# Four single PSUM banks instead of two bank pairs for the down products of a Strassen-style SwiGLU

## The chip, the cores and the metric

The kernel runs on one core of one Trainium2 chip. The metric is the device time of one execution, in microseconds (us). Three runs of the kernel before gave 1541.43, 1543.85 and 1544.39 us, so the median is 1543.85 us.

## The reference, cut to what matters

The program is one decoder layer on 1024 tokens of width 1024: modulation from a condition vector, a mixer of sparse attention and causal pooling, a layer norm, a gated feed-forward (SwiGLU) and a second layer norm. The change lies in the feed-forward:

```python
def swiglu(h, w_gate, w_up, w_down):
    return (jax.nn.silu(h @ w_gate) * (h @ w_up)) @ w_down

x = layer_norm(ALPHA * x + gate2 * ffn, ln2_g[l], ln2_b[l])
```

The hidden width is 2816, which is 11 times 256.

## The kernel before

**Operands.** All matrix work has float32 quality: an operand is split into a high part (rounded by ScalarE) and a low part (the rest, subtracted on VectorE or GpSimd), and a product is three matmuls, high by high, high by low and low by high (the table `SPLITS`).

**Passes.** The feed-forward goes over the 11 groups of 256 hidden columns. Line 1544 is the loop of the nine middle passes, `for p in range(1, NFP - 1)`. A pass computes the gate products ("g") of group p, the down products ("d") of group p-1, and the up products ("u") of group p. Each of the three is done as a two-by-two block product in seven steps instead of eight, in the manner of Strassen and Winograd. The sums of blocks that this needs are formed on GpSimd and VectorE. I write g0 to g6, d0 to d6 and u0 to u6 for the steps. The order in which a pass is written down is the string on line 60, `DOWN_AT = "gdgdgdggdgdgdd"`, followed by the seven up steps:

```
g0 d0 g1 d1 g2 d2 g3 g4 d3 g5 d4 g6 d5 d6   u0 u1 u2 u3 u4 u5 u6
```

**A gate or up step** (`gu_step`, line 1376) is 12 matmuls into a single PSUM bank of the pool `ps1` (four banks, tiles named `gu`). Step 3 is split into two halves of six, around step 4.

**A down step** (`down_step`, line 1526) is four groups of three matmuls. Group i (0 to 3) takes 128 tokens of the activations and writes bank i. Behind each group VectorE adds bank i to a tile of the residual, `res_X` (an evacuation of 128x512). Steps d0, d2, d4 and d6 start fresh sums (the flag `new` in the table `DOWN` on line 1288). Steps d1, d3 and d5 go on summing in the banks of the step before them, after that step's sums have been read out:

```python
DOWN = (("A11", "B11", True, (22,)), ("A12", "B21", False, (11,)), ("S1", "T1", True, (22,)), ("A22", "T4", False, (-21,)),
        ("S3", "T3", True, (22,)), ("S4", "B22", False, (-12,)), ("S2", "T2", True, (22,)))
```

**The banks before.** The four banks come as two tiles of 1024 columns from the pool `ps2` (two buffers, `psB` on line 213). Groups 0 and 1 share the first tile, groups 2 and 3 the second. A matmul that writes a tile is made to wait for the VectorE read of that tile that stands ahead of it in the program, whichever half of the tile it read.

**Weights.** A step's weights are a block of 128x1024 (high and low part) in one of four slots, used in turn (`wblk_V` and `wblk_T`, two each). A block is made up to four steps ahead (`LEAD = 4`), and a slot is free when the matmuls that read it are done. The raw weights of a gate, down or up group lie in one of two buffers, `wraw_R` and `wraw_W`. When the last block of a group has been made, the SyncE queue issues the load of the group after next into the same buffer (`load_set`).

**Activations.** The u steps end in the seven operands of the next down steps, `act_W` and `act_R`, again high and low part (`act_split`, line 1370).

**Order.** In the attention stages the order on three engines is fixed by the program. From line 975 on (`pinned.clear()`) it is not: the build orders each engine's instructions by the dependencies and its own estimates. All of what follows lies behind that line. Every operation is issued through one helper, so the profile shows L159 for nearly all of them, and they are told apart by the names of their tiles: `dn` is a down sum, `gu` a gate or up sum.

Of the kernel before, what the change touches and what calls it, by code (L numbers as in the profile page):

```python
# [171 lines left out]
def decoder_layer_kernel(  # L172
# [16 lines left out]
        area[nm_] = at  # L189
        at += 4 * words  # L190
    nc.alloc_sbuf_tensor("arena", [P, (at - nc.sbuf_base) // 4], F32)
    ps2 = ctx.enter_context(tc.tile_pool(name="ps2", bufs=2, space=bass.MemoryType.PSUM))
    ps1 = ctx.enter_context(tc.tile_pool(name="ps1", bufs=4, space=bass.MemoryType.PSUM))

    def buf(where, off, n, name, dt=F32):
        return nc.alloc_sbuf_tensor_at(f"{name}_{where}{off}", [P, n], dt, offset=area[where] + 4 * off).ap()

    n_ps = [0]

    ps_ring = {"ps1": [], "ps2": []}  # L200

    def ps_tile(pool, tag, n, depth, nm):
        n_ps[0] += 1
        t = pool.tile([P, n], F32, tag=tag, name=f"{nm}_{n_ps[0]}")
        ring = ps_ring[tag]
        times.prev[t[:, 0:n].name] = ring[-depth] if len(ring) >= depth else None
        ring.append(t[:, 0:n].name)
        return t
# [4 lines left out]
    def psB(nm="pb"):  # L213
        return ps_tile(ps2, "ps2", 1024, 2, nm)
# [725 lines left out]
    for n_, (kind, a, b) in enumerate(groups):  # L940
        if n_ in PAIRS:
            pb = psB("pair")
# [184 lines left out]
    for n_, u in enumerate(units):  # L1127
        g, pr, i = u
# [178 lines left out]
    def block(n):  # L1307
        if n < 7:
            return FIRST[n]
        if n < len(blocks) - 8 or n >= len(blocks) - 4:  # L1310
            return RING[(n - 7) % NRING]
        return TOK[:, 1, n + 8 - len(blocks)]
# [50 lines left out]
    def use_blocks(n):  # L1363
        pos["used"] += n

        lead = LEAD + 4 if pos["used"] >= len(blocks) - 11 else LEAD
        while pos["made"] < min(pos["used"] + lead, len(blocks)):
            make_block()
# [63 lines left out]
    def gate_up(kind, act, after=None):  # L1432
        for n in range(7):
            gu_step(kind, n, 0, 4, act)
            if after is not None:
                after(n)
# [63 lines left out]
    def E(rc, i):  # L1500

        t = 7 - 2 * i if rc >= 20 else 6 - 2 * i
        return XR[t][:, 0:512] if rc % 10 == 1 else XR[t][:, 512:1024]
# [3 lines left out]
    def affine(n=0):  # L1507
        if todo:
            t = todo.pop(0)
            V.tensor_tensor(XR[t], XR[t], GR, ALU.mult)  # L1510
            (G if t in AFF_G else V).tensor_tensor(XR[t], XR[t], lnb, ALU.add)
            if t % 2 == 0:
                for to in (12, 21):
                    G.tensor_tensor(E(to, (7 - t) // 2), E(to, (7 - t) // 2), E(22, (7 - t) // 2), ALU.subtract)
            if not todo:
                SP.dma_start(GR, g2_d.to_broadcast([P, 1024]))
# [4 lines left out]
            affine()  # L1521
    gate_up("u", ACTS, lambda n: affine())

    bank = {}

    def down_step(p, n):
        a_, w_, new, (to,) = DOWN[n]
        wd_ = block(pos["used"])
        if new:
            pb = [psB("dn"), psB("dn")]  # L1530
            bank.update({i: pb[i // 2][:, (i % 2) * 512 : (i % 2 + 1) * 512] for i in range(4)})
        for i in range(4):
            for m, (a, b) in enumerate(SPLITS):
                T.matmul(bank[i], ACTS[a_][:, a * 512 + i * P : a * 512 + (i + 1) * P], wd_[:, b * 512 : (b + 1) * 512],
                         start=(new and m == 0), stop=(m == 2), skip_group_check=True)
            z = E(abs(to), i)
            op = ALU.add if to > 0 else ALU.subtract
            if p == 0 and (n == 0 or not new):
                V.scalar_tensor_tensor(z, z, float(np.float32(ALPHA)), bank[i], ALU.mult, op)
            else:  # L1540
                V.tensor_tensor(z, z, bank[i], op)
        use_blocks(1)

    for p in range(1, NFP - 1):
        n_g = n_d = 0
        for kind in DOWN_AT:
            if kind == "g":
                gu_step("g", n_g, 0, 4, None)
                n_g += 1
            else:  # L1550
                down_step(p - 1, n_d)
                n_d += 1
        gate_up("u", ACTS if p < NFP - 2 else PLAIN)
# [109 lines left out]
```

## Time and profile before

| what | value |
|---|---|
| median of three runs | 1543.85 us |
| time of the profiled execution | 1548.71 us |
| its span, first to last instruction | 1546.8 us |
| TensorE matmuls, busy | 1262.8 us (82%) |
| VectorE busy | 1059.8 us (69%) |
| GpSimd busy | 821.5 us (53%) |
| ScalarE busy | 609.6 us (39%) |
| mean granted TensorE clock | 0.893 |

Busy time is a sum over the whole span, and says nothing of which engine is waited for at a given place. For that one reads the waits (who waited for whom), the timeline (instructions of one engine in order of time, with the idle time ahead of each in square brackets and what ended it) and the chain of work that ended last. PE is TensorE, DVE is VectorE, ACT is ScalarE, POOL is GpSimd. The granted clock is a share of full speed.

### The profile page before, as it was taken

To read this page: it belongs to the slowest core of one execution; us is meant where nothing else is said; L and a number is where in the kernel's file an instruction comes from. 1 tells how busy PE (TensorE), PEld (TensorE's weight loads), DVE (VectorE), ACT (ScalarE), POOL (GpSimd) and SP (SyncE) were. 2 spreads that over 40 slices of the span, in tenths; PEclk is the share of its full clock that TensorE was granted. 3 is DMA by queue.
4 is the path that set the end of the run, shared out by engine and by line. 5 is a ranking of instruction groups with operands and counts; after the bars stand their busy time and mean duration, and the time that the engine had idled before them with its cause. 6 is when DMAs were issued, how large, how long until landed. Compare 5 with 4: busy or idle time off the path is not lost.

```text
span 1546.8 us, 16019 instructions
## 1 busy us (share of the span) xinstructions
PE 1262.8 (82%) x5462; PEld 965.7 (62%) x5462; DVE 1059.8 (69%) x1725; ACT 609.6 (39%) x1141; POOL 821.5 (53%) x779
## 2 busy tenths in 40 slices
PE   7888978677699799947787878787969696969886
PEld 6655666565366478746665656575757574747675
DVE  6898898999779847874555646464555555645478
ACT  2446516456577644633222232222323222323321
POOL 1573847574344532595455555545464646465547
PEclk9999989898699889968797979797979797979989
DMA  9520113010006641011110101010101020202012
GB/s 351 188 96 14 66 37 102 22 68 21 0 15 199 234 133 41 1 52 57 30 53 28 55 28 55 28 55 25 58 11 72 4 78 1 82 1 82 28 55 109
DMA packets 24999, 101.80 MB, mean 66 GB/s; under 512 B 3411, under 2 KB 3411, under 8 KB 20566
## 3 DMA queue, kind: packets, MB, share of 16 engines
q1 hardware_dynamic: 24918, 100.78, 18.4%
q8 instruction: 43, 0.70, 0.2%
q14 instruction: 38, 0.31, 0.1%
HBM read 92.38 MB, written 8.40 MB: 65 GB/s over the span
## 4 chain that ended last, share of the span: by engine, by line
PE 30%; DVE 27%; POOL 22%; issue 9%; DMA 6%; ACT 6%; SPq 0%; DVEq 0%; POOLq 0%; ACTq 0%
PE gu L159 13%; PE dn L159 11%; DVE junk_X L159 7%; POOL act_W L159 4%; POOL wraw_R L159 4%; POOL wraw_W L159 3%; DVE score_X L159 3%; DVE stat_C L159 2%; POOL res_X L159 2%; DMA wraw_R<-in_wd_dram 2%; DVE res_X L159 2%; PE o L159 2%; PE pT L159 2%; DMA wraw_W<-in_wd_dram 2%; POOL gtmp_V L159 1%
## 5 line engine op out<-in xcount | busy, mean ns | idle before, releaser
L159 PE MATMUL gu<-hr_H,wblk_V 128*128 128x512 f32 (+1 forms) x936 | 244.3, 407 | 22.2 <-POOL hr_H L159 13.2
L159 PE MATMUL gu<-hr_H,wblk_T 128*128 128x512 f32 (+1 forms) x924 | 235.1, 402 | 5.8 <-ACT gtmp_V L159 3.0
L159 PEld LDWEIGHTS gu<-hr_H,wblk_V 128*128 128x128 f32 x936 | 185.4, 202 | 63.0 <-POOL hr_H L159 13.7
L159 DVE TENSOR_TENSOR res_X<-res_X,dn 128x512 f32<-128x512 f32 (+1 forms) x253 | 169.7, 683 | 70.6 <-PE dn L159 70.3
L159 PEld LDWEIGHTS gu<-hr_H,wblk_T 128*128 128x128 f32 x924 | 180.9, 201 | 44.2 <-ACT gtmp_V L159 3.4
L159 PE MATMUL dn<-wblk_V,act_W 128*128 128x512 f32 x324 | 99.1, 440 | 74.2 <-DVE res_X L159 52.8
L159 PE MATMUL dn<-wblk_T,act_W 128*128 128x512 f32 x324 | 97.3, 436 | 60.7 <-DVE res_X L159 43.3
L159 PE MATMUL pj<-ws_W,hT_H 128*128 128x512 f32 x456 | 124.7, 422 | 18.7 <-DVE kr_K L159 6.5
L159 PEld LDWEIGHTS dn<-wblk_V,act_W 128*128 128x128 f32 x324 | 64.4, 209 | 101.4 <-DVE res_X L159 65.4
L159 POOL TENSOR_TENSOR wraw_R<-wraw_R 128x512 f32<-128x512 f32 x64 | 90.9, 1421 | 57.2 <-DVE wblk_T L159 23.1
L159 PEld LDWEIGHTS dn<-wblk_T,act_W 128*128 128x128 f32 x324 | 64.7, 208 | 86.3 <-DVE res_X L159 54.3
L159 PEld LDWEIGHTS pj<-ws_W,hT_H 128*128 128x128 f32 x456 | 88.9, 201 | 46.4 <-issue 16.7
L159 POOL TENSOR_TENSOR wraw_W<-wraw_W 128x512 f32<-128x512 f32 x60 | 82.5, 1375 | 46.9 <-DVE wblk_T L159 23.0
L159 POOL TENSOR_SCALAR sm_H<-sm_H,stat_X 128x1024 f32<-128x1024 f32 (+7 forms) x64 | 58.3, 923 | 73.7 <-DVE stat_X L159 58.4
L159 DVE TENSOR_TENSOR act_W<-gtmp_V,act_W 128x512 fp32r<-128x512 f32 x19 | 23.3, 1225 | 89.2 <-ACT act_W L159 89.2
L159 DVE TENSOR_SCALAR_CACHE_REDUCE junk_X<-keysD_T,colsD_X 128x1024 int16<-128x1024 int16 (+1 forms) x64 | 78.9, 1269 | 0.8
L159 ACT ACTIVATE wblk_V<-wraw_R 128x512 fp32r<-128x512 f32 x56 | 35.3, 632 | 101.8 <-PE dn L159 42.3
L159 ACT ACTIVATE wblk_V<-wraw_W 128x512 fp32r<-128x512 f32 x54 | 34.1, 631 | 100.3 <-PE dn L159 38.3
L159 ACT ACTIVATE wblk_T<-wraw_W 128x512 fp32r<-128x512 f32 x55 | 34.6, 630 | 95.8 <-PE dn L159 40.0
L159 ACT ACTIVATE act_W<-gtmp_V 128x512 fp32r<-128x512 f32 x48 | 29.3, 627 | 101.5 <-POOL gtmp_V L159 81.4
L159 ACT ACTIVATE wblk_T<-wraw_R 128x512 fp32r<-128x512 f32 x53 | 33.2, 630 | 88.3 <-PE dn L159 34.9
L159 POOL TENSOR_TENSOR wraw_R<-wraw_R,gr_G 128x512 f32<-128x512 f32 x24 | 32.9, 1380 | 62.1 <-DMA wraw_R<-in_wd_dram 62.1
(300 smaller groups left out, 2864.8 us busy)
## 6 DMA issues: line engine op xcount, KB each, us to landing
wm_K<-in_wma_dram SPq DMA_DIRECT2D x16, 512.0 KB, 8.8
modraw_V<-in_wmc_dram SPq DMA_DIRECT2D x16, 512.0 KB, 4.5
wraw_R<-in_wg_dram SPq DMA_DIRECT2D x6, 1024.0 KB, 4.8
wraw_R<-in_wd_dram SPq DMA_DIRECT2D x6, 1024.0 KB, 4.7
wraw_W<-in_wup_dram SPq DMA_DIRECT2D x6, 1024.0 KB, 4.7
modraw_V<-in_wmg_dram SPq DMA_DIRECT2D x10, 512.0 KB, 4.5
wraw_R<-in_wup_dram SPq DMA_DIRECT2D x5, 1024.0 KB, 4.7
wraw_W<-in_wg_dram SPq DMA_DIRECT2D x5, 1024.0 KB, 4.7
```

The costliest lines, as they stand in the source:

```text
L159: ins_ = f(*a, **k)
```

## The change

The pools are opened in another order, the pair pool `ps2` is closed before the first down step, and a new pool `ps3` of four single banks takes its place. The down step takes four tiles of 512 columns where it took two of 1024. `DOWN_AT`, the arithmetic and the tiles of every other stage stay as they are.

```diff
-    ps2 = ctx.enter_context(tc.tile_pool(name="ps2", bufs=2, space=bass.MemoryType.PSUM))
     ps1 = ctx.enter_context(tc.tile_pool(name="ps1", bufs=4, space=bass.MemoryType.PSUM))
+    pairs = ExitStack()
+    ps2 = pairs.enter_context(tc.tile_pool(name="ps2", bufs=2, space=bass.MemoryType.PSUM))
...
-    ps_ring = {"ps1": [], "ps2": []}
+    ps_ring = {"ps1": [], "ps2": [], "ps3": []}
...
+    pairs.close()
+    ps3 = ctx.enter_context(tc.tile_pool(name="ps3", bufs=4, space=bass.MemoryType.PSUM))
     bank = {}
...
         if new:
-            pb = [psB("dn"), psB("dn")]
-            bank.update({i: pb[i // 2][:, (i % 2) * 512 : (i % 2 + 1) * 512] for i in range(4)})
+            bank.update({i: ps_tile(ps3, "ps3", 512, 4, "dn") for i in range(4)})
         for i in range(4):
             for m, (a, b) in enumerate(SPLITS):
                 T.matmul(bank[i], ACTS[a_][:, a * 512 + i * P : a * 512 + (i + 1) * P], wd_[:, b * 512 : (b + 1) * 512],
                          start=(new and m == 0), stop=(m == 2), skip_group_check=True)
```

The build orders TensorE anew in all nine passes. ScalarE and SyncE keep their order row for row, GpSimd has only four sums behind the last pass in another order, and VectorE keeps its rows except for which bank an evacuation reads. The rows below are of the first pass, and the other eight repeat the pattern.

TensorE of before, at the start of a pass. `dn_5268` is the first pair (groups 0 and 1), `dn_5269` the second (groups 2 and 3). `gu_5290` belongs to g1, and the later `gu_5251` to g2:

```order
L159 MATMUL dn_5268<-wblk_V_4094,act_W_4103 128x512 x3
L159 MATMUL dn_5269<-wblk_V_4094,act_W_4103 128x512 x3
L159 MATMUL gu_5290<-hr_H_2677,wblk_V_4095 128x512 x3
L159 MATMUL dn_5268<-wblk_V_4094,act_W_4103 128x512 x3
L159 MATMUL gu_5290<-hr_H_2677,wblk_V_4095 128x512 x2
L159 MATMUL dn_5269<-wblk_V_4094,act_W_4103 128x512 x3
L159 MATMUL gu_5290<-hr_H_2677,wblk_V_4095 128x512 x7
L159 MATMUL dn_5268<-wblk_T_4096,act_W_4105 128x512 x3
L159 MATMUL dn_5269<-wblk_T_4096,act_W_4105 128x512 x3
L159 MATMUL gu_5251<-hr_H_2677,wblk_T_4097 128x512 x3
L159 MATMUL dn_5268<-wblk_T_4096,act_W_4105 128x512 x3
L159 MATMUL dn_5269<-wblk_T_4096,act_W_4105 128x512 x3
```

The groups of d0 and d1 stand in the order 0, 2, 1, 3, and matmuls of g1 and g2 stand between them.

TensorE of the changed kernel at the same place. `dn_5272` to `dn_5275` are banks 0 to 3, `gu_5296` is g1 and `gu_5255` is g2:

```order
L159 MATMUL dn_5272<-wblk_V_4094,act_W_4103 128x512 x3
L159 MATMUL dn_5273<-wblk_V_4094,act_W_4103 128x512 x3
L159 MATMUL dn_5274<-wblk_V_4094,act_W_4103 128x512 x3
L159 MATMUL dn_5275<-wblk_V_4094,act_W_4103 128x512 x3
L159 MATMUL gu_5296<-hr_H_2677,wblk_V_4095 128x512 x12
L159 MATMUL dn_5272<-wblk_T_4096,act_W_4105 128x512 x3
L159 MATMUL dn_5273<-wblk_T_4096,act_W_4105 128x512 x3
L159 MATMUL dn_5274<-wblk_T_4096,act_W_4105 128x512 x3
L159 MATMUL dn_5275<-wblk_T_4096,act_W_4105 128x512 x3
L159 MATMUL gu_5255<-hr_H_2677,wblk_T_4097 128x512 x12
```

Each step now stands in one piece: the 12 matmuls of d0, the 12 of g1, the 12 of d1, the 12 of g2.

VectorE of before at the evacuations of d0. `res_X_4080`, `4078`, `4076` and `4074` are the residual tiles of groups 0, 1, 2 and 3, and `act_W_4104` is the low part of the operand S4:

```order
L159 SCALAR_TENSOR_TENSOR res_X_4080<-res_X_4080,dn_5268 128x512
L159 TENSOR_TENSOR act_W_4104<-gtmp_V_4111,act_W_4104 128x512
L159 SCALAR_TENSOR_TENSOR res_X_4076<-res_X_4076,dn_5269 128x512
L159 SCALAR_TENSOR_TENSOR res_X_4078<-res_X_4078,dn_5268 128x512
L159 SCALAR_TENSOR_TENSOR res_X_4074<-res_X_4074,dn_5269 128x512
```

VectorE of the changed kernel at the same place:

```order
L159 SCALAR_TENSOR_TENSOR res_X_4080<-res_X_4080,dn_5272 128x512
L159 TENSOR_TENSOR act_W_4104<-gtmp_V_4111,act_W_4104 128x512
L159 SCALAR_TENSOR_TENSOR res_X_4078<-res_X_4078,dn_5273 128x512
L159 SCALAR_TENSOR_TENSOR res_X_4076<-res_X_4076,dn_5274 128x512
L159 SCALAR_TENSOR_TENSOR res_X_4074<-res_X_4074,dn_5275 128x512
```

The five rows stand at the same place in the queue. The third row now reads the bank of group 1, where it read that of group 2.

TensorE of before at the end of the down steps, d5 (`dn_5433`, `dn_5434`), d6 (`dn_5489`, `dn_5490`) and the 12 matmuls of u0 (`gu_5509`):

```order
L159 MATMUL dn_5433<-wblk_T_4097,act_W_4104 128x512 x3
L159 MATMUL dn_5434<-wblk_T_4097,act_W_4104 128x512 x3
L159 MATMUL gu_5509<-hr_H_2677,wblk_V_4095 128x512 x4
L159 MATMUL dn_5433<-wblk_T_4097,act_W_4104 128x512 x3
L159 MATMUL dn_5434<-wblk_T_4097,act_W_4104 128x512 x3
L159 MATMUL gu_5509<-hr_H_2677,wblk_V_4095 128x512
L159 MATMUL dn_5489<-wblk_V_4094,act_W_4108 128x512 x3
L159 MATMUL dn_5490<-wblk_V_4094,act_W_4108 128x512 x3
L159 MATMUL gu_5509<-hr_H_2677,wblk_V_4095 128x512 x3
L159 MATMUL dn_5489<-wblk_V_4094,act_W_4108 128x512 x3
L159 MATMUL dn_5490<-wblk_V_4094,act_W_4108 128x512 x3
L159 MATMUL gu_5509<-hr_H_2677,wblk_V_4095 128x512 x4
```

TensorE of the changed kernel there:

```order
L159 MATMUL dn_5441<-wblk_T_4097,act_W_4104 128x512 x3
L159 MATMUL dn_5442<-wblk_T_4097,act_W_4104 128x512 x3
L159 MATMUL dn_5443<-wblk_T_4097,act_W_4104 128x512 x3
L159 MATMUL dn_5444<-wblk_T_4097,act_W_4104 128x512 x3
L159 MATMUL dn_5499<-wblk_V_4094,act_W_4108 128x512 x3
L159 MATMUL dn_5500<-wblk_V_4094,act_W_4108 128x512 x3
L159 MATMUL dn_5501<-wblk_V_4094,act_W_4108 128x512 x3
L159 MATMUL dn_5502<-wblk_V_4094,act_W_4108 128x512 x3
L159 MATMUL gu_5521<-hr_H_2677,wblk_V_4095 128x512 x12
```

d5 and d6 stand back to back, and all 12 matmuls of u0 stand behind them.

## The prediction

> **What bounds the kernel now.** I read the page first, then the waits, then TensorE's timeline over one pass, then the chain of work that ended last. The waits name what TensorE waits for in the down steps (in total, times, longest):
>
> ```profile
> PE dn L159 <- DVE res_X L159: 96.2, 27, 6.7
> ```
>
> That is 27 waits of a down matmul for an evacuation, 96.2 us in all, or three waits in each of the nine passes. TensorE's timeline shows where they stand. I take the third pass as the example; columns are start, duration, and in brackets the idle time ahead:
>
> ```profile
> 882.38 0.61 PE L159 MATMUL dn<-wblk_T,act_W 128*128 128x512 f32 x2
> 887.35 1.65 PE L159 MATMUL dn<-wblk_T,act_W 128*128 128x512 f32 x4 [4.35 <-POOL act_W L159]
> ...
> 896.76 1.65 PE L159 MATMUL dn<-wblk_T,act_W 128*128 128x512 f32 x3 [6.48 <-DVE res_X L159]
> ...
> 903.08 1.65 PE L159 MATMUL dn<-wblk_T,act_W 128*128 128x512 f32 x3 [3.81 <-DVE res_X L159]
> 904.52 3.19 PE L159 MATMUL gu<-hr_H,wblk_T 128*128 128x512 f32 x7
> ...
> 909.96 1.52 PE L159 MATMUL dn<-wblk_V,act_W 128*128 128x512 f32 x6
> 911.32 2.20 PE L159 MATMUL gu<-hr_H,wblk_V 128*128 128x512 f32 x9
> ```
>
> Step d0 starts at 882.38, waits 4.35 us for a low part from GpSimd, and runs groups 0 and 2. Group 1 then waits 6.48 us and group 3 another 3.81 us, each for an evacuation of its bank pair. From 903.08 on TensorE runs without a wait but for one of 0.63 us (quoted below). So 903.08 is the point from which the pass is dense; I call it X. What sets X is in the chain of work that ended last:
>
> ```profile
> 868.72 0.64 ACT wblk_V L159
> 869.39 0.70 DVE wblk_V L159
> 870.15 4.78 DMA wraw_R<-in_wd_dram
> ...
> 899.81 1.23 POOL gtmp_V L159
> 901.07 0.64 ACT act_W L159
> 901.73 0.69 DVE act_W L159
> 902.42 0.61 DVE res_X L159
> ```
>
> The chain is a ring. TensorE frees a weight slot in the up steps (868.7), ScalarE and VectorE make the last up block, its buffer takes the load of the next down weights (870.15), GpSimd works through a queue that begins when the load lands and ends with the sum for S4 (899.81), ScalarE and VectorE split S4 (901.73), and the evacuation behind that split in VectorE's queue releases TensorE at X. A dense stretch of TensorE closes the ring. The passes repeat it, the first and the last of nine X being:
>
> ```profile
> 745.15 1.65 PE L159 MATMUL dn<-wblk_V,act_W 128*128 128x512 f32 x3 [3.81 <-DVE res_X L159]
> 1374.46 1.65 PE L159 MATMUL dn<-wblk_V,act_W 128*128 128x512 f32 x3 [3.81 <-DVE res_X L159]
> ```
>
> That is 78.66 us a pass (629.31 / 8). TensorE is not at full speed all the time. The stretches of the third pass with their granted clock (the column of 1.00 or less behind the POOL column):
>
> ```profile
> 882.99:887.35 4.36, 0.01 (x2) 0.01 (x1) 3.90 (x4) 0.92 (x2) 4.36 (x4) 1.00 0.00 0
> 887.35:890.28 2.93, 2.93 (x7) 1.80 (x7) 0.49 (x1) 1.15 (x2) 2.93 (x3) 0.59 0.00 0
> ...
> 903.08:907.50 4.42, 4.42 (x10) 3.48 (x11) 1.22 (x2) 0.81 (x2) 1.95 (x2) 0.50 0.01 4
> 907.50:909.28 1.78, 1.78 (x8) 1.42 (x6) 1.19 (x2) 0.45 (x1) 1.70 (x2) 0.77 0.00 0
> 909.28:941.16 31.88, 31.25 (x135) 24.66 (x134) 21.09 (x32) 9.53 (x16) 10.84 (x9) 1.00 0.18 66
> ```
>
> After the 4.36 us idle the clock is halved, and it is still at 0.50 for the first 4.42 us after X. A mean of 0.77 over the next 1.78 us puts the return to full speed 0.82 us in, near 908.3. At half clock a matmul takes 0.442 us (10 in 4.42 us), at full clock 0.227 us (909.96 to 911.32, six).
>
> **The change, part by part.** *Pools and banks.* Opening the pools in another order issues nothing; no instruction is added or removed, and the four reordered GpSimd sums lie behind the last pass. I price this at nothing, in nine passes and in the tail.
>
> *The wait for the other half of a pair goes.* The 12 matmuls of d0 no longer wait for each other's evacuations, and the 12 of g1 follow. At 887.35 there remain 10 of d0 and 12 of g1, 22 matmuls: 5.0 us at full clock, 9.7 us at half, so TensorE is through by 892.3 at the earliest and 897.1 at the latest. Next is group 0 of d1, which goes on in bank 0 and needs bank 0 evacuated and its operands made:
>
> ```profile
> 892.66 1.78 DVE L159 TENSOR_TENSOR act_W<-gtmp_V,act_W 128x512 fp32r<-128x512 f32 x1 [4.82 <-ACT act_W L159]
> ...
> 896.03 0.67 DVE L159 TENSOR_TENSOR res_X<-res_X,dn 128x512 f32<-128x512 f32 x1
> ```
> ```profile
> 893.86 1.71 POOL L159 TENSOR_TENSOR wblk_V<-wraw_R,wblk_V 128x512 fp32r<-128x512 f32 x1
> ```
>
> The low part of A12 is there at 894.4, the block's low part at 895.6, the evacuation at 896.7. So group 0 of d1 runs between 896.7 and about 898.4. Group 1 of d1 needs the evacuation of bank 1. That evacuation now has the place in VectorE's queue that the one of group 2 had, behind the S4 split, and ends at the same 903.03. So X stays where it was: the wait moves from d0 to d1, and nothing ahead of X gets faster, because GpSimd's queue sets it.
>
> *What is left after X.* Before, from X to the end of d1 with three matmuls of g2 done (911.32), TensorE had 25 to run by the order of its rows: 3 of d0, 7 of g1, 12 of d1, 3 of g2. Now 12 are left: 9 of d1 and 3 of g2. The difference is 13. The half-clock stretch of 5.2 us stays, and holds some 12 matmuls in either kernel, so the 13 come off the full-speed part: 13 x 0.227 = 2.95 us a pass. Check: from 903.08 at 0.442, 12 matmuls end near 908.4, against 911.32. The evacuations of banks 2 and 3 follow at 0.61 us each while a group at half clock takes 1.3 us, so groups 2 and 3 don't wait.
>
> *The end of the down steps.* Before, d5 had a wait, with this chain ahead of it:
>
> ```profile
> 930.54 0.64 ACT wblk_T L159
> 931.21 0.70 DVE wblk_T L159
> ...
> 931.98 1.30 POOL wraw_W L159
> 933.30 0.64 ACT wblk_V L159
> 933.97 1.22 DVE wblk_V L159
> 935.19 0.61 DVE res_X L159
> 935.84 1.66 PE dn L159 x6
> ```
> ```profile
> 935.84 1.66 PE L159 MATMUL dn<-wblk_V,act_W 128*128 128x512 f32 x6 [0.63 <-DVE res_X L159]
> ```
>
> When d4 is done with its slot, ScalarE and VectorE make u0's block, GpSimd forms a sum, u1's block is made, and only then does VectorE evacuate d5's group 0: 5.3 us from 930.5 to 935.8. The 0.63 us wait of d5's group 1 goes. A new wait can take its place: d6's group 0 writes bank 0, nothing of u0 stands ahead of it any more, and behind it in TensorE's queue is everything of u0. From d4's end TensorE has g6 and d5 to run, 24 x 0.227 = 5.4 us, against the chain's 5.3. VectorE must first add g6's sum, which ends 0.2 us later than before, so I take a new wait of 0.1 us. Its bounds are 0 and 1.6 us, the latter if three VectorE operations of that chain are stretched as the 1.22 us one is against its neighbour of 0.70 us. In the other steps a group takes 3 x 0.227 = 0.68 us and an evacuation 0.61, and 12 gate matmuls (2.7 us) or two steps lie between a bank's reading and its next use: nothing.
>
> *The sum.* 2.95 + 0.63 - 0.1 = 3.48 us a pass, bounds 2.0 (with the 1.6 us wait) and 3.6 (with none). Nine passes: 31.3 us, bounds 18 and 32. All of it lies on the ring, since X is a fixed time behind the slot freed in the up steps. The last stages move along whole, and may gain or lose one half-clock stretch (2.6 us) by where the clock changes fall. The profiled execution would come to 1548.71 - 31.3 = 1517.4 us; it lies 4.86 us above the median of the runs, so the forecast is 1512.6 us for the median.
>
> [...]
>
> **The rivals.** *Slower: the back-to-back d5 and d6.* Before, the build had put 11 matmuls of u0 between the groups of d5 and d6, which hid the evacuations; now there are none. If the chain that ends in d5's evacuation gets longer (the sum on GpSimd, or the up weights that land before it), TensorE stands at d6 with all of u0 behind it. It decides from 3.5 us on. A wait as long as the longest quoted, 6.48 us, would cost 3.0 us net a pass, 27 us in all: 1571 us. Against it speaks that this chain took 5.3 us before and is not changed but for the order of one sum. 0.08.
>
> *No change: the ring doesn't follow TensorE.* If the load of the down weights, or GpSimd, had its own pace of 78.66 us, TensorE would come earlier to d0 and wait there longer than 4.35 us, and the time would stay at 1543.9 us. For it speaks that GpSimd's queue sets X. Against it: the load at 870.15 is issued right behind the block that waited for TensorE's slot. 0.06.
>
> *Faster still: the clock stays up.* Between 887.35 and 898.4 TensorE is now nearly without a gap, and if the clock came back there and outlasted the idle stretch up to X, the 5.2 us after X would run at full speed: 2.6 us a pass more, 23 us, 1489 us. Against it: the idle stretch is about 4.7 us at least (898.4 to 903.08), and the one of 4.36 us in the rows halved the clock. 0.06. [...]
>
> **How the numbers follow.** The forecast has the remaining 0.80, with 1512.6 us and, from its bounds (18 and 32 us) and the clock in the tail, 1508 to 1528 us. The range for 8 in 10 leaves out the rivals and reaches 2 us further down, 1506 to 1528. A measurement of this kernel tells about 0.2% (3 us) from no change. Faster by more than that: 0.80 + 0.06 = 0.86; within it 0.06; slower 0.08.
>
> **What would show it.** In the changed profile d0 has only the GpSimd wait; d1 has a wait of 4.7 us or more ahead of its group 1, still released by an evacuation, and at most a short one ahead of group 0; X stands 34.4 us behind the ScalarE row that starts the ring (868.72 here); the distance from X to X is about 75.2 us; the wait in d5 is gone, and d6 has none above 1.6 us. The forecast is wrong if TensorE shows a new wait between d1 and u0, if d0's GpSimd wait grows by what the dense stretch loses, or if the distance from X to X stays near 78.7 us.

## The result, and the profile after it

The changed kernel takes 1505.67 us (median of 4 runs, 1505.17 to 1510.02), the kernel before 1544.12 us (median of 4, 1541.43 to 1547.4). The ratio is 0.9756, with an interval of 0.973 to 0.9783: 38.45 us less. The forecast was 1512.6 us, so the sign and the place were right and the size was 7 us too small; the time lies 0.3 us under the low end of the range. The profiled execution of the changed kernel took 1506.04 us, its span is 1504.1 us.

First the waits of TensorE's down matmuls for an evacuation (in total, times, longest), in the changed kernel:

```profile
PE dn L159 <- DVE res_X L159: 67.1, 18, 5.3
```

Of 27 waits 18 are left, of 96.2 us 67.1. TensorE's timeline over the third pass shows where they are now:

```profile
871.77 4.11 PE L159 MATMUL dn<-wblk_T,act_W 128*128 128x512 f32 x10 [4.41 <-POOL act_W L159]
875.68 2.97 PE L159 MATMUL gu<-hr_H,wblk_T 128*128 128x512 f32 x12
881.35 0.93 PE L159 MATMUL dn<-wblk_V,act_W 128*128 128x512 f32 x3 [2.71 <-DVE res_X L159]
887.57 4.21 PE L159 MATMUL dn<-wblk_V,act_W 128*128 128x512 f32 x9 [5.28 <-DVE res_X L159]
891.58 3.55 PE L159 MATMUL gu<-hr_H,wblk_V 128*128 128x512 f32 x12
```

d0 has only its GpSimd wait, 4.41 us where it was 4.35. Then d0 and g1 run through, 22 matmuls in 6.88 us (871.77 to 878.65). The waits now stand in d1: 2.71 us ahead of group 0 and 5.28 us ahead of group 1. X is 887.57 in this pass. What sets it is in the chain of work that ended last, from the slot that TensorE frees in the up steps on:

```profile
853.11 0.64 ACT wblk_V L159
853.75 0.02 issue
853.77 0.70 DVE wblk_V L159
...
854.54 4.84 DMA wraw_R<-in_wd_dram
...
884.31 1.23 POOL gtmp_V L159
885.54 0.02 issue
885.56 0.64 ACT act_W L159
```

It is the same ring: load, GpSimd's queue down to S4's sum, ScalarE, VectorE, evacuation. X comes 34.46 us behind the ScalarE row that starts it (887.57 - 853.11), against 34.36 before. The ring's first part has the length it had, and the gain lies in the dense stretch behind X. These are the stretches from X to the end of u0, first in the kernel before and then in the changed kernel (the number ahead of the comma is the length of the stretch, the one behind it PE's busy time, with its matmuls; the granted clock is the number behind POOL's column):

```profile
903.08:942.07 38.99, 38.36 (x154) 30.30 (x155) 24.39 (x36) 11.42 (x19) 14.50 (x11) 0.93 0.15 55
```
```profile
887.57:922.49 34.92, 34.88 (x142) 28.30 (x142) 24.49 (x37) 10.42 (x18) 14.56 (x12) 0.92 0.17 61
887.57:892.85 5.28, 5.28 (x12) 4.13 (x13) 4.66 (x8) 0.78 (x2) 5.12 (x4) 0.50 0.00 0
```

38.99 against 34.92 us: 4.07 us less in this pass, with the same 5.3 us or so at half clock. The timeline's rows from X up to the first matmul of u1 add up to 154 matmuls before and 141 now (the view's 142 counts the first one of u1 in), so the 13 are there: 13 x 0.227 = 2.95 us. The other 1.1 us are lost time within and between the steps that is gone; it is counted below, behind the second experiment and in the account of the prediction.

The last such stretch in the changed kernel, d5, d6 and u0:

```profile
914.01 2.88 PE L159 MATMUL dn<-wblk_V,act_W 128*128 128x512 f32 x12
916.93 3.00 PE L159 MATMUL dn<-wblk_T,act_W 128*128 128x512 f32 x12
919.77 2.88 PE L159 MATMUL gu<-hr_H,wblk_T 128*128 128x512 f32 x12
```

Steps that follow one another without a gap start 2.72 us apart, as d6's neighbours further up do. d6 starts 2.92 us behind d5, so the new wait is 0.2 us, and u0 starts 2.84 us behind d6, so another 0.12 us are lost inside d6.

Finally the first, the eighth and the ninth X:

```profile
739.53 3.80 PE L159 MATMUL dn<-wblk_T,act_W 128*128 128x512 f32 x9 [5.29 <-DVE res_X L159]
...
1262.18 4.21 PE L159 MATMUL dn<-wblk_V,act_W 128*128 128x512 f32 x9 [5.29 <-DVE res_X L159]
...
1337.22 3.63 PE L159 MATMUL dn<-wblk_T,act_W 128*128 128x512 f32 x9 [5.28 <-DVE res_X L159]
```

Eight passes take 597.69 us, 74.71 each, where they took 629.31 us. So the profiled executions' 42.67 us (1548.71 - 1506.04) come in three pieces: 5.62 us ahead of the first X (745.15 against 739.53), 31.62 us in the eight passes, and 5.43 us behind the ninth X (174.25 us to the end before, 168.82 now), the ninth dense stretch among it. The first piece is hardly the change's: it is there already where the first d0 goes on after its GpSimd wait (723.73 against 729.41), ahead of any evacuation of a down product, and the profiled execution of before lies 4.59 us above its median, about as much. The same place comes at 724.69 in a run below that keeps the pairs (the last one), and at 728.35 in one with single banks (the sixth), so it moves from execution to execution.

### The profile page after: what moved, and what is told of

Read it like the earlier page. It is cut to its first block, busy times and chain, and to the rows that moved or that the text cites. A ratio compares the mean times of both kernels' runs of the same rounds, so it can differ in the third digit from the quotient of the medians.

```text
span 1504.1 us, 16028 instructions
## 1 busy us (share of the span) xinstructions
PE 1250.9 (83%) x5462; PEld 969.2 (64%) x5462; DVE 1057.8 (70%) x1725; ACT 609.1 (40%) x1141; POOL 823.8 (55%) x779
## 4 chain that ended last, share of the span: by engine, by line
PE 33%; DVE 25%; POOL 22%; issue 8%; ACT 6%; DMA 6%; DVEq 0%; SPq 0%; POOLq 0%; ACTq 0%
PE gu L159 14%; PE dn L159 13%; DVE junk_X L159 5%; POOL act_W L159 4%; POOL wraw_R L159 4%; POOL wraw_W L159 3%; DVE score_X L159 3%; DVE stat_C L159 2%; POOL res_X L159 2%; DMA wraw_R<-in_wd_dram 2%; DVE res_X L159 2%; DMA wraw_W<-in_wd_dram 2%; PE pT L159 2%; POOL gtmp_V L159 1%; PE o L159 1%
## 5 line engine op out<-in xcount | busy, mean ns | idle before, releaser
L159 PE MATMUL gu<-hr_H,wblk_V 128*128 128x512 f32 (+1 forms) x936 | 228.3, 396 | 21.4 <-POOL hr_H L159 13.3
L159 PE MATMUL gu<-hr_H,wblk_T 128*128 128x512 f32 (+1 forms) x924 | 222.6, 395 | 5.8 <-ACT gtmp_V L159 3.0
L159 PEld LDWEIGHTS gu<-hr_H,wblk_V 128*128 128x128 f32 x936 | 180.7, 197 | 60.6 <-POOL hr_H L159 13.8
L159 DVE TENSOR_TENSOR res_X<-res_X,dn 128x512 f32<-128x512 f32 (+1 forms) x253 | 164.0, 679 | 53.1 <-PE dn L159 52.8
L159 PEld LDWEIGHTS dn<-wblk_T,act_W 128*128 128x128 f32 x324 | 70.0, 221 | 77.1 <-DVE res_X L159 28.6
L159 PEld LDWEIGHTS dn<-wblk_V,act_W 128*128 128x128 f32 x324 | 70.8, 224 | 74.4 <-POOL act_W L159 23.7
L159 ACT ACTIVATE wblk_V<-wraw_W 128x512 fp32r<-128x512 f32 x54 | 34.0, 630 | 90.1 <-PE gu L159 32.3
```

The costliest lines, as they stand in the source:

```text
L159: ins_ = f(*a, **k)
```

## The experiments

The theory to be tested: the single banks act at two separate places of a pass, at its start (13 matmuls come ahead of X) and in the later steps (waits go), and X itself is set by S4's sum in GpSimd's queue, which neither kernel changes. The first rival: it is the order of TensorE's instructions, not the banks, that gave the gain. The second: X is set by something else in the ring, the load or the evacuations.

**The start alone.** Single banks for d0 and d1, pairs for the other steps.

```diff
-            bank.update({i: ps_tile(ps3, "ps3", 512, 4, "dn") for i in range(4)})
+            bank.update(sums("single" if n == 0 else "pair"))
```

Here `sums` is a helper of this run, which closes one pool and opens the other at each change between single banks and pairs.

> Single banks for d0 and d1 alone; d2 to d6 keep the pairs and their interleaving. Theory (the wait for the pair's other half goes, 13 matmuls come ahead of X, and the pass closes a ring through TensorE): 13 x 0.227 = 2.95 us a pass less, from 78.66 to 75.7 us between two X, nine times 27 us, about 1517 us; the 0.63 us wait in d5 stays. If instead the gain comes from the later steps standing in one piece: 78.7 us a pass and 1544 us. [...]

Measured: 1513.29 us, ratio 0.9811 (0.9791 to 0.9832) to 1542.34 us of the kernel before in the same comparison: 29.1 us less. The waits in d0 are gone as in the changed kernel; the one in d5 is there as before:

```profile
919.44 1.67 PE L159 MATMUL dn<-wblk_V,act_W 128*128 128x512 f32 x6 [0.60 <-DVE res_X L159]
```

The start is worth most of the gain, close to the 9 x 2.95 = 26.6 us that the prediction had for it. The clock has a part in it, too. In the third pass it is 35.37 us from X to the end of u0 (890.29 to 925.66), 3.62 us less than before; 2.95 of these are the 13 matmuls, and most of the rest is a half-clock stretch of 3.7 us in place of 5.3. From the first X to the ninth a pass takes 75.18 us, and not the 75.7 that the expectation worked out from the matmuls alone.

**The rest alone.** Pairs for d0 and d1, single banks for d2 to d6.

```diff
+            bank.update(sums("single" if n > 0 else "pair"))
```

> The complement: d0 and d1 keep the pairs, d2 to d6 have single banks. Theory: the waits of 6.2 and 3.8 us in d0 stay, X stays where it was, and only the 0.63 us wait in d5 and waits too short to be listed go: 0.6 to 1.1 us a pass, 5 to 10 us in all, 1534 to 1539 us. If the later steps carry the gain: near 1506 us.

Measured: 1530.8 us, ratio 0.9924 (0.9906 to 0.9942): 11.5 us less. The waits in d0 stay, and two of the later steps read:

```profile
887.50 1.65 PE L159 MATMUL dn<-wblk_T,act_W 128*128 128x512 f32 x3 [6.06 <-DVE res_X L159]
...
893.81 1.65 PE L159 MATMUL dn<-wblk_T,act_W 128*128 128x512 f32 x3 [3.81 <-DVE res_X L159]
...
903.57 2.88 PE L159 MATMUL dn<-wblk_T,act_R 128*128 128x512 f32 x12
...
917.17 2.88 PE L159 MATMUL dn<-wblk_T,act_W 128*128 128x512 f32 x12
```

The two parts add up, within what the clock puts in: 29.1 + 11.5 = 40.6 us, against 38.45 for the whole change. But the rest is worth 11.5 us, and the prediction's terms for it, (0.63 - 0.1) x 9, are 4.8. What it missed stands in TensorE's rows of the kernel before:

```profile
913.36 1.52 PE L159 MATMUL dn<-wblk_T,act_R 128*128 128x512 f32 x6
914.72 0.39 PE L159 MATMUL gu<-hr_H,wblk_T 128*128 128x512 f32 x1
914.98 1.66 PE L159 MATMUL dn<-wblk_T,act_R 128*128 128x512 f32 x6
916.48 1.31 PE L159 MATMUL gu<-hr_H,wblk_T 128*128 128x512 f32 x5
```

Read the starts: the first six matmuls of d2 take 1.36 us to the next row's start (913.36 to 914.72), the second six 1.50 (914.98 to 916.48). 0.14 us are lost inside the second six, too short for the view to show as idle time. The same stands in d4, d5 and d6 (0.14, 0.14 and 0.16), together 0.58 us a pass in which nothing is marked as waiting. The one wait that is marked, 0.63 us in d5, is 0.78 us from start to start: 1.69 us from 934.15 to 935.84, with four matmuls of 0.227 in between. Where the steps stand in one piece, their 12 matmuls take 2.72 us (12 x 0.227).

**The pairs in the written order.** The kernel before, with TensorE held to the order in which the code is written.

```diff
+    pinned.add("T")
     for p in range(1, NFP - 1):
...
+    pinned.discard("T")
```

> The pairs of before, but TensorE held to the written order in the nine passes, so each down step stands in one piece as in the changed kernel. Theory (the banks matter, the order only hides them): group 1 waits for group 0's evacuation and group 3 for group 2's with the next gate step behind them, some 0.9 us each in d1 to d6, that is 10 us a pass, and group 3 of d0 with all of g1 comes behind X, 1 us more: near 88 us a pass, about 1630 us. If the order of TensorE were what brings the gain: near 1506 us.

Measured: 1694.79 us in one run, against 1542.34: 152 us more. The waits in total, times, longest, and rows of the third pass:

```profile
PE dn L159 <- DVE res_X L159: 218.9, 126, 8.9
```
```profile
935.91 1.65 PE L159 MATMUL dn<-wblk_T,act_W 128*128 128x512 f32 x3 [3.99 <-DVE res_X L159]
...
949.54 0.84 PE L159 MATMUL dn<-wblk_T,act_R 128*128 128x512 f32 x3
951.16 1.65 PE L159 MATMUL dn<-wblk_T,act_R 128*128 128x512 f32 x6 [0.78 <-DVE res_X L159]
953.59 0.96 PE L159 MATMUL dn<-wblk_T,act_R 128*128 128x512 f32 x3 [0.78 <-DVE res_X L159]
```

With pairs, the down steps wait twice for 0.78 us or more: after three matmuls, and after six more. So group 1 starts only when group 0 has been evacuated out of the other half of the same pair, and group 3 when group 2 has. The written order is what the single banks give: the changed kernel stands in it on TensorE. So the order alone loses 152 us, and the order with single banks gains 38: the first rival falls. The loss is larger than the expected 87 us. The third pass takes 95.15 us in place of 88, from d0's restart at 919.61 to the next at 1014.76. Its twelve waits in d1 to d6 add up to 11.7 us, and its two in d0 to 12.9, where the pairs in the order of before have 10.3 (6.48 + 3.81). The order that the build had found for the pairs was a way around their waits, and it left the pieces of 0.14 us.

**The third gate step ahead of the second down step.** The table of the order is changed, on single banks. In this kernel d2 stands between g3 and g4, where the code takes the weights by position, so d2 reads g3's weights in place of its own, and part of what it computes is other than the reference's; the number and the size of the instructions are the same.

```diff
-DOWN_AT = "gdgdgdggdgdgdd"
+DOWN_AT = "gdggdgdgdgdgdd"
```

> The changed kernel with g2 written ahead of d1 (g0 d0 g1 g2 d1 g3 d2 g4 d3 ...), so that 12 more matmuls run in the idle stretch ahead of X. Theory: X stays behind GpSimd's queue, 12 x 0.227 = 2.7 us a pass come off what is left behind it: 75.0 to 72.3 us a pass, 24 us in all, about 1481 us. If the pass is paced by GpSimd or the load of the weights and not through TensorE: 1506 us, with a longer wait ahead of d0. If d1 to d2 now stand too close (only six matmuls between them) for the evacuations: a new wait at d2 and less than half of the 24 us.

Measured: 1490.91 us, ratio 0.9663 (0.9645 to 0.9682). But g2 doesn't run ahead of the restart; it is the restart:

```profile
870.21 4.02 PE L159 MATMUL dn<-wblk_T,act_W 128*128 128x512 f32 x10 [4.38 <-POOL act_W L159]
...
882.69 1.27 POOL L159 TENSOR_TENSOR wblk_V<-wraw_R,wblk_V 128x512 fp32r<-128x512 f32 x1
882.76 0.63 ACT L159 ACTIVATE act_W<-gtmp_V 128x512 fp32r<-128x512 f32 x1 [5.48 <-POOL gtmp_V L159]
883.30 0.58 ACT L159 ACTIVATE gtmp_V<-gu 128x512 f32<-128x512 f32 x1
...
883.93 4.91 PE L159 MATMUL gu<-hr_H,wblk_V 128*128 128x512 f32 x12 [6.83 <-ACT gtmp_V L159]
```

ScalarE's copy of g0's sum (883.30) stands behind S4's split (882.76) in its queue, and g2 needs the bank that the copy frees. What moved is S4: it is split 12.55 us behind the start of d0, where it took 13.79 us in the changed kernel (885.56 - 871.77), 1.24 us less. One GpSimd operation fewer stands ahead of its sum: the low part of d1's weights is behind it now (882.69 above), where the changed kernel has it ahead:

```profile
878.36 1.71 POOL L159 TENSOR_TENSOR wblk_V<-wraw_R,wblk_V 128x512 fp32r<-128x512 f32 x1
```

TensorE restarts 13.72 us behind the start of d0 (883.93 - 870.21) in place of 15.80 (887.57 - 871.77), with three more matmuls left to run: 2.08 - 0.68 = 1.40 us a pass, 12.6 us in nine. So a gain of 15 us came, of the expected 24, and it came from a restart that is earlier, not from more work ahead of it.

**S4's sum on VectorE.** The sum that the theory says sets X is taken out of GpSimd's queue, on single banks.

```diff
-SUM_G = ("S2", "S3", "S4")
+SUM_G = ("S2", "S3")
```

> Single banks as in the changed kernel, and S4's sum of each pass taken from GpSimd to VectorE. Theory (each pass restarts when S4's sum has come out of GpSimd's queue): in the third pass VectorE is free right behind A12's low part, some 3.1 us before GpSimd's sum ended, so ScalarE's copy, the split, the evacuation and the restart X move up by about 3.1 us; GpSimd gets nine sums fewer. Nine passes by about 3.1 us are 28 us, so about 1478 us; passes of 71.7 to 72 us in place of 75.05. Rival (the restart is set by the load of weights or by the ring as a whole, GpSimd's sum being merely last by little): 1506 us, or up to 1.7 us a pass slower, 1521 us, since VectorE carries the sums now.

Measured: 1472.07 us (1471.3 to 1475.57), ratio 0.9537 (0.9505 to 0.9568) to 1544.24 us of the kernel before: 72.2 us less, and 33.6 less than the changed kernel. The third pass, around the restart:

```profile
864.90 4.15 PE L159 MATMUL dn<-wblk_T,act_W 128*128 128x512 f32 x10 [4.25 <-POOL act_W L159]
...
872.18 1.56 DVE L159 TENSOR_TENSOR gtmp_V<-gtmp_V,gtmp_V 128x512 f32<-128x512 f32 x1
...
873.77 0.63 ACT L159 ACTIVATE act_W<-gtmp_V 128x512 fp32r<-128x512 f32 x1 [2.83 <-DVE gtmp_V L159]
...
875.34 0.67 DVE L159 TENSOR_TENSOR res_X<-res_X,dn 128x512 f32<-128x512 f32 x1
...
876.16 5.79 PE L159 MATMUL dn<-wblk_V,act_W 128*128 128x512 f32 x12 [4.35 <-ACT wblk_T L159]
```

The sum begins 7.3 us behind the start of d0 (872.18 - 864.90) instead of 12.5 us (884.31 in the chain above - 871.77), S4's split comes 8.87 us behind it instead of 13.79, and d1 has one wait of 4.35 us in place of 2.71 and 5.28 (the view names ScalarE, but what it wrote is the block of a later step; d0's first evacuation on VectorE ends at 876.01, just ahead of d1, and in the first pass the view names it). X is the start of d1 here. From the first X (735.38) to the ninth (1302.12) a pass takes 70.84 us. The gain is above the expected 28 us: X comes 11.26 us behind the start of d0 in place of 15.80, with three matmuls more left behind it, so 4.54 - 0.68 = 3.86 us a pass, 34.7 us in nine. The second rival falls as far as the way from d0 to X goes: with the same d0 and the same evacuations X comes earlier once the sum is out of GpSimd's queue. The load still stands ahead of d0 in the ring, where the wait for GpSimd stays at 4.25 us.

**The third gate step earlier, with the next two adjacent.** As the fourth experiment, with an order that keeps g3 and g4 together.

```diff
-DOWN_AT = "gdgdgdggdgdgdd"
+DOWN_AT = "gdggddggdgdgdd"
```

> Single banks as in the changed kernel, and the third gate step put ahead of the second down step, with the next two gate steps adjacent behind the third down step. Theory (the restart is set by S4's sum on GpSimd): the gate step does not run ahead of the restart, since its buffer waits for ScalarE's copy, which stands behind S4's; but the low part of the second down step's weights moves behind S4's sum in GpSimd's queue, so the sum comes 1.3 to 2 us earlier a pass: about 1490 us. Rival (the gate step's 12 matmuls fill the gap ahead of the restart, 12 by 0.227 is 2.7 us a pass): about 1481 us. Second rival (two down steps back to back make TensorE wait for an evacuation): about 1506 us.

Measured: 1492.91 us, ratio 0.967 (0.9641 to 0.9698), the theory's number. g2 waits as it did in the fourth:

```profile
888.47 5.49 PE L159 MATMUL gu<-hr_H,wblk_V 128*128 128x512 f32 x12 [5.58 <-ACT gtmp_V L159]
```

**Both.** S4's sum on VectorE and the order of the sixth.

```diff
-SUM_G = ("S2", "S3", "S4")
-DOWN_AT = "gdgdgdggdgdgdd"
+SUM_G = ("S2", "S3")
+DOWN_AT = "gdggddggdgdgdd"
```

> Both edits at once: S4's sum on VectorE and the third gate step ahead of the second down step, single banks. If both work by bringing S4's sum forward in a queue, the second has little left to bring once the sum isn't on GpSimd: what it gives is the gate step's work before the restart, about 1.7 us a pass at most beyond the run with S4's sum on VectorE alone: about 1463 us if that run gives 1478, and no less than that run's time if the gate step still waits for ScalarE.

Measured: 1478.19 us, ratio 0.9567 (0.953 to 0.9604); the interval overlaps that of S4's sum on VectorE alone. The 1463 us did not come, and g2 still waits for ScalarE:

```profile
885.48 5.30 PE L159 MATMUL gu<-hr_H,wblk_V 128*128 128x512 f32 x12 [5.06 <-ACT gtmp_V L159]
```

This fits an order that had helped by moving S4's sum forward: once the sum is off GpSimd it has nothing left to give.

**The pairs with S4's sum on VectorE.** The kernel before, with the same one-line edit of `SUM_G`.

> The pairs of banks of the kernel before, with S4's sum on VectorE. Theory (banks and S4's sum act at separate places of a pass and add): some 28 us less than the kernel before, about 1516 us, and the banks' gain of 38 us stands between this run and the single banks with S4's sum on VectorE. Rival (the pairs' evacuation, not the sum, sets the restart): the time of the kernel before, 1544 us, within 5 us.

Measured: 1511.92 us, ratio 0.9787 (0.9761 to 0.9814): 32.3 us less than before. The pairs keep their waits, a longer one in d0 and one in d1:

```profile
885.88 1.65 PE L159 MATMUL dn<-wblk_T,act_W 128*128 128x512 f32 x3 [7.31 <-DVE res_X L159]
...
894.26 1.67 PE L159 MATMUL dn<-wblk_V,act_W 128*128 128x512 f32 x6 [0.80 <-DVE res_X L159]
```

S4's sum is worth 32.3 us with pairs and 33.6 with single banks, and the banks are worth 38.45 us with the sum on GpSimd and 39.85 with it on VectorE (1511.92 - 1472.07). Within 1.4 us they are two separate terms of a pass.

## Why the prediction came out as it did

**X stays behind GpSimd's queue: right.** 34.46 us behind the ring's start, forecast 34.4. That the sum in this queue sets X, and not something beside it, is shown by moving S4's sum: 33.6 us.

**13 matmuls come ahead of X: right.** The rows show 141 in place of 154 matmuls from X to u1, and the single banks at the start alone gave 29.1 us, forecast 26.6, with some help of the clock.

**d1's waits: one right, one too small.** Group 1 waits 5.28 us, forecast 4.7 or more. Group 0 was to have at most a short wait and has 2.71, because TensorE was through d0 and g1 after 6.88 us. It costs nothing, since X follows.

**The end of the down steps: right in kind, too small.** d5's marked wait is gone, d6 starts 0.2 us late, forecast 0.1 with a bound of 1.6. The rival that was to end slower had its place here, and had no more than that 0.2 us. The term was 0.63 - 0.1 = 0.53 us a pass. From start to start the marked wait was 0.78 us, the pieces in d5 and d6 were 0.14 and 0.16, and the changed kernel loses 0.20 and 0.12 at d6: 0.76 us.

**"In the other steps ... nothing": wrong.** This is the step that failed. The prediction compared an evacuation of 0.61 us with a group of 0.68, and looked for listed waits. The pieces of 0.14 us in d2 and d4 were in the quoted timeline's neighbouring rows, in the distance from one start to the next, 0.28 us a pass. So 3.48 us a pass should have been 2.95 + 0.76 + 0.28 = 3.99, and from X to the end of u0 it measured 4.07. Nine passes of this are 36.6 us; from the first X to the end the profiled executions differ by 37.05 (31.62 + 5.43), forecast 31.3. That the later steps alone are worth more than the 4.8 us of the forecast was measured directly, with single banks for them alone: 11.5 us. Of that the rows account for 0.76 + 0.28 = 1.04 us a pass, 9.4 us in all. The rest, 2.1 us, is about what the clock gave in that run: read in slices of 1 us, its half-clock stretches behind the nine X are 4.6 us in the mean, before 5.2, and half of the difference in nine passes is 2.7 us. In the changed kernel the mean is 5.1, so over the whole change the clock has next to no part: it gave time in some passes and took it in others, as the distances from X to X below show.

**The load follows TensorE, the clock stays down: right.** d0's GpSimd wait did not grow (4.41 against 4.35), so the rival of no change is out. The clock is 0.50 for 5.28 us behind X, so the rival of a clock that stays up is out too. The idle stretch ahead of it was 5.28 us long, and the clock was at 0.50 when it ended.

**The distance from X to X.** Forecast 75.2 us; it is 74.71 in the mean and 75.04 from the eighth X to the ninth. The distance is no constant in either kernel, since the half-clock stretch behind X changes from pass to pass, where the prediction had taken it as fixed at 5.2 us. These are the stretches behind the first and the eighth X in the kernel before:

```profile
745.15:753.15 8.00, 8.00 (x22) 6.31 (x23) 3.30 (x5) 1.26 (x2) 5.45 (x4) 0.61 0.01 2
1296.05:1304.05 8.00, 8.00 (x25) 6.42 (x26) 3.65 (x6) 1.26 (x2) 5.45 (x4) 0.70 0.01 2
```

A mean of 0.61 over 8.00 us is 6.2 us at half clock, and 0.70 is 4.8. The first pass takes 79.08 us (745.15 to 824.23) and the eighth 78.41 (1296.05 to 1374.46). In the changed kernel it goes the other way:

```profile
739.53:743.53 4.00, 4.00 (x11) 3.20 (x12) 3.79 (x7) 0.31 (x2) 3.84 (x3) 0.60 0.00 0
743.53:745.53 2.00, 2.00 (x11) 1.64 (x10) 2.00 (x2) 0.47 (x1) 1.51 (x2) 1.00 0.00 0
```
```profile
1262.18:1268.36 6.18, 6.18 (x15) 4.84 (x16) 5.42 (x8) 0.78 (x2) 5.34 (x4) 0.50 0.00 0
```

A mean of 0.60 over 4.00 us is 3.2 us at half clock behind the first X; behind the eighth it is 6.18. Each microsecond at half clock loses about half a microsecond of work (0.442 us a matmul against 0.227), so the eighth pass should be (6.18 - 3.2) / 2 = 1.5 us longer than the first, which was 73.61 us (739.53 to 813.14): 75.1. The third pass, which the prediction took as its example, is one in which the two kernels have this stretch alike (5.3 us), so the 4.07 us there are the edit's own.

The last four distances are 78.52 us in the mean before and 75.02 in the changed kernel, 3.50 us apart. That the prediction's sum of 3.48 us comes so near to this is luck: the edit is worth 4.07 us a pass, and a half-clock stretch that is 6.1 us in these passes, before 4.9, took 0.6 of it back.

## What to carry to other kernels

Count lost time from start to start, not from the list of waits: pieces of 0.14 us, four to a pass, were worth 0.58 us here, against 0.78 for the one wait that was listed. Where two groups shared one tile of sums in this build, the second waited for the evacuation of the first (6.48 and 3.81 us in d0 of the third pass before), so try a tile of its own for every group that is evacuated on its own before tuning the order around the waits. And when a wait goes, ask what sets the next one: here it was still one sum in GpSimd's queue, and moving it was worth another 33.6 us.

## What the runs showed of the hardware

**Two kernels came out at one distance from X to X.** With single banks at the start alone, the edit is worth about 1 us less a pass than the whole change, and yet the last three passes have the same length within 0.2 us (75.14, 75.16 and 74.98 us against 74.99, 75.00 and 75.04). Its eighth X, and the clock behind it:

```profile
1265.90 3.99 PE L159 MATMUL dn<-wblk_V,act_W 128*128 128x512 f32 x9 [5.28 <-DVE res_X L159]
```
```profile
1265.90:1269.90 4.00, 4.00 (x10) 3.18 (x11) 3.62 (x6) 0.14 (x1) 3.84 (x3) 0.55 0.00 0
```

The ninth X comes at 1340.88, 74.98 us later. The half-clock stretch behind X is 3.6 us (a mean of 0.55 over 4.00) where the changed kernel has 6.18: the 2.6 us difference is worth 1.3 us of work, about what the edit lacks. So in this pass of the changed kernel about 1.3 us of the gain in the dense stretch was taken back by a later return of the clock. Two other runs show no such distance: single banks in the later steps alone gave distances from 76.96 to 77.96 us, and S4's sum on VectorE from 69.97 to 71.49. What makes these two agree was not tried.

**The pairs' price depends on the order.** The same pairs of banks cost 38 us in the order that the build found for them and 189 us in the written one (1694.79 - 1505.67).
